# Reordering VectorE and ScalarE work at the first pairs, the half changes and the launch, and making a half's first weight sums within the output projection before it

## The chip, the cores and the metric

The kernel runs on one core of a Trainium2 chip. Its time is the time of one launch on the device, in microseconds. TensorE (PE) does the matrix products, VectorE (DVE) and ScalarE (ACT) prepare their operands and read their results, GpSimd (POOL) takes a few additions, SyncE (SP) issues the loads of the weights. Each engine works through its own list of instructions in the order in which they are written; what has to wait there holds all that stands behind it.

## The reference

One decoding step of a two-layer trunk, for 512 prompt tokens and 64 sample tokens that share all weights (576 tokens, width 1024, everything in float32). Cut to the parts that the change touches:

```python
D_MODEL, D_FF, DEPTH = 1024, 2816, 2

def rms_norm(x, g):
    return x * lax.rsqrt(jnp.mean(x * x, axis=-1, keepdims=True) + EPS) * g

def swiglu(x, w_gu, w_down):
    g, u = jnp.split(x @ w_gu, 2, axis=-1)
    return (jax.nn.silu(g) * u) @ w_down

for l in range(DEPTH):
    x += 0.5 * swiglu(rms_norm(x), w_gu_1, w_down_1)        # half 0, half 2
    if l % 2 == 0:
        x += concat(attention(norm x), pooling(norm x)) @ w_o   # mixer of layer 0
    else:
        x += (Bg * conv3(Cg * v)) @ w_out                   # mixer of layer 1
    x += 0.5 * swiglu(rms_norm(x), w_gu_2, w_down_2)        # half 1, half 3
y = rms_norm(x)
```

So four feed-forward halves are run, in the order half 0, attention mixer, half 1, half 2, convolution mixer, half 3, final norm.

## The kernel before

**Numbers.** Tokens lie on the free axis, as two column halves of 288. A float32 operand is split into a high part (ACT: a cast, L100 for weights, L240 for activations) and a low part (DVE: source minus high part, L101, L241), and a product is made as three: high by high, high by low, low by high. A row of weights can't be used before both its cast on ACT and its difference on DVE are there.

**A unit** (`unit`, one 128-wide slice of gate and up) is done in a Strassen-like form with seven block products instead of eight. They are called B11, T1, B21, B22, T2, T3 and T4 after the form of x that they use, each of twelve matmuls 128x288 (`seven`, L381). B11 and B21 use the raw weights (group "a"), T1 and T2 use the group "e", T3 and B22 the group "f". "e" and "f" are made from sums of weight blocks: three DVE additions, L111 to L113 (`Weights.sums`), then a split each. T4 uses weights split by `dsplit` (tiles dh, dl). It is run in the next unit, once its result bank B has been read by the gate products: the DVE operations L387 and L388 make h from it, and T4 waits for L387. The copy of T2's result (tile u, ACT L475 in the first unit of a chunk) has to be done before T3 writes into the same bank.

**Forms of x.** The products need B11, T1, B21, B22, T2, T3, T4 of x: sums and differences of quarters of x, multiplied by the norm's gain and split. `forms_low` makes those of a row d below 4, `forms_high` and `form_b22` and `forms_main` those of the row d+4. The sum of squares of x for the norm is collected beside them by `square` (ACT L285 squares, POOL L286 adds).

**Order.** 22 units of a half are run in four chunks of 5, 5, 6 and 6. After each chunk's units come eight down projections in the order 0, 4, 1, 5, 2, 6, 3, 7, and x is updated row by row. In the last chunk of a half that is followed by another half, and in the output projection of a mixer, each update of x (L650, L787, L1005) is followed by the forms of the next half. `W.ahead(n)` issues the splits of the next n weight groups at the place where it stands. Groups "e" and "f" need a tile for the sum, `spool`, which before exists only within a half's own pools (`ffn_pools`). So at the two output projections the splits stop short of the first "e".

**Where engines meet.** A chunk's first unit (`unit` with `prev` None) has no unit before it whose products could fill the time in which its operands are made. The first unit of a half is also marked `start`: the norm's factor is made there, `tok_factor` on PE (L327), a square root on ACT (L331), `newton` and `factor_tiles` on DVE, and a turn on PE (L346).

**Launch.** In half 0 the first three units are done in the plain form (`first_pairs`, `plain`, L494), while the forms for the seven products are still made; `late_form` makes T4's form for four rows after the first unit in seven products.

Of the kernel before, what the change touches and what calls it, by code (L numbers as in the profile page):

```python
# [32 lines left out]
C = 288  # L33
# [13 lines left out]
class Weights:  # L47
# [5 lines left out]
    def __init__(self, nc, raw_pool, split_pool, units):  # L53
# [12 lines left out]
        self.spool = self.dpool = None  # L66
# [36 lines left out]
    def sums(self, u):  # L103
# [4 lines left out]
        t = self.sum[u] = self.spool.tile([128, 2048], F32, tag="sum", name="sum")  # L108
# [6 lines left out]
    def split(self):  # L115
# [3 lines left out]
        if k in ("e", "f") and self.spool is None:  # L119
            return  # L120
# [52 lines left out]
class Trunk:  # L173
# [63 lines left out]
    def hi_lo(self, hl, src, g):  # L237

        nc = self.nc
        nc.scalar.activation(out=hl[0], in_=src, func=AF.Copy, scale=g)  # L240
        nc.vector.scalar_tensor_tensor(out=hl[1], in0=src, scalar=g, in1=hl[0].bitcast(F32), op0=ALU.mult, op1=ALU.subtract)  # L241
# [10 lines left out]
    def forms_high(self, k, n, xb, st):  # L252

        ng = self.ngain[:, n, k + 4:k + 5]
        self.form_b21(k, n)
        self.form_t32(k, n, xb, st)
        self.nc.vector.scalar_tensor_tensor(out=st[:, 2], in0=self.x[:, k + 4, :C], scalar=ng, in1=st[:, 1], op0=ALU.mult, op1=ALU.subtract)

    def form_b21(self, k, n):
        self.hi_lo(self.form("B21", k), self.x[:, k + 4, :C], self.gain[:, n, k + 4:k + 5])  # L260
# [10 lines left out]
    def forms_main(self, k, st):  # L271

        n = st.shape[1]
        h, l = (t[:, k, 1:1 + n, :] for t in self.mn)
        self.nc.scalar.copy(out=h, in_=st)
        self.nc.vector.tensor_tensor(out=l, in0=st, in1=h.bitcast(F32), op=ALU.subtract)
# [127 lines left out]
    def unit(self, u, j, prev, fresh, start, pre):  # L404
# [31 lines left out]
        if prev:  # L436
# [19 lines left out]
            return s  # L456
        we = W.take()
# [38 lines left out]
    def plain(self, j, outs, mid={}):  # L496
# [18 lines left out]
    def first_pairs(self, n):  # L515
# [6 lines left out]
        tmp = lambda: tp.tile([128, C], F32, tag="t1", name="t1")  # L522
# [5 lines left out]
        for i, j in ((0, 1), (2, 3), (4, 5), (6, 7), (4, 6), (0, 2), (0, 4)):  # L528
            nc.vector.tensor_tensor(out=sq[i], in0=sq[i], in1=sq[j], op=ALU.add)
        self.hidden_tiles()  # L530
        W.ahead(1)

        def sums(ks):
            for k in ks:
                xb, st = tmp(), tp.tile([128, 3, C], F32, tag="st", name="st")[:, :2]
                nc.scalar.activation(out=xb, in_=self.x[:, k, C:], func=AF.Copy, scale=self.gain[:, n, k:k + 1])
                self.form_t32(k, n, xb, st)
                self.forms_main(k, st)

        (g0, g1), (u0, u1) = p0  # L540
        fa = []
# [1014 lines left out]
```

## Time and profile before

| | |
|---|---|
| median of 3 runs | 2380.42 us (2378.46 to 2380.97) |
| profiled execution | 2382.45 us, its span 2380.6 us |
| mean granted clock of TensorE | 0.971 |
| PE busy | 2239.2 us, 94% |
| DVE, ACT, POOL busy | 1625.9, 928.8, 431.4 us |

A span is the time from the first to the last instruction in the trace. PE is the busiest engine; what the other engines do costs only where PE waits for it. The clock is given as a share of full speed: 1.0 is 2.4 GHz, 0.50 is 1.2 GHz.

### The profile page before, as it was taken

How to read it: one execution, taken by the hardware profiler on the slowest of the kernel's cores; microseconds unless marked ns; L12 is line 12 of the kernel's file. 1: busy time of each engine (PE TensorE's matmuls, PEld its weight loads, DVE VectorE, ACT ScalarE, POOL GpSimd, SP SyncE). 2: the span in 40 equal slices, each digit the busy share in tenths (PEclk: the TensorE clock that was granted, in tenths of full speed). 3: DMA queues.
4: the chain of work that ended last, by engine and by line, in shares of the span. 5: the costliest groups of instructions: out<-in, count | busy, mean ns of one | idle time of the engine just before them, and what ended most of it. 6: DMA issues, size and time to landing. Idle time of an engine off the chain costs nothing.

```text
span 2380.6 us, 39876 instructions
## 1 busy us (share of the span) xinstructions
PE 2239.2 (94%) x16544; PEld 2186.2 (92%) x16544; DVE 1625.9 (68%) x2600; ACT 928.8 (39%) x1606; POOL 431.4 (18%) x444
## 2 busy tenths in 40 slices
PE   8799999999999979999998799999999989999998
PEld 7799999899888879999998799999999989999998
DVE  6676767635667777668596767767664467768584
ACT  5343524323434335334354534343431245335253
POOL 0000101207556530000011001000222210000012
PEclk9899999999999999999999799999999989999999
DMA  3122222443444412222222122222222212222222
GB/s 130 62 83 87 80 91 83 153 137 113 129 134 137 129 54 76 93 81 89 89 85 76 54 88 79 100 89 72 89 90 89 73 54 87 82 98 85 78 88 75
DMA packets 70949, 217.89 MB, mean 92 GB/s; under 512 B 14256, under 2 KB 37808, under 8 KB 54128
## 3 DMA queue, kind: packets, MB, share of 16 engines
q1 hardware_dynamic: 70336, 215.24, 27.3%
q8 instruction: 130, 2.13, 0.4%
q14 instruction: 51, 0.42, 0.1%
q10 hardware_dynamic: 432, 0.10, 0.0%
HBM read 204.22 MB, written 11.10 MB: 90 GB/s over the span
## 4 chain that ended last, share of the span: by engine, by line
PE 47%; DVE 12%; ACT 4%; issue 2%; POOL 0%; POOLq 0%; ACTq 0%; DVEq 0%
PE B L381 11%; PE acc L362 9%; PE A L579 7%; PE F L579 7%; PE F L381 7%; PE A L381 6%; DVE wl L101 2%; ACT wh L100 2%; DVE sum L111 1%; DVE sum L112 1%; DVE exl L241 1%; DVE sum L113 1%; DVE dl L101 1%; DVE x L650 1%; ACT sqt L285 0%
## 5 line engine op out<-in xcount | busy, mean ns | idle before, releaser
L101 DVE TENSOR_TENSOR wl<-raw,wh 128x1024 fp32r<-128x1024 f32 (+3 forms) x305 | 336.2, 1108 | 145.9 <-ACT wh L100 145.7
L100 ACT CAST wh<-raw 128x1024 fp32r<-128x1024 f32 (+3 forms) x305 | 278.6, 916 | 324.2 <-PE F L579 201.7
L402 POOL TENSOR_TENSOR hl<-h,hh 128x576 fp32r<-128x576 f32 x88 | 134.3, 1526 | 1435.6 <-ACT hh L401 1383.5
L101 DVE TENSOR_TENSOR wl<-sum,wh 128x1024 fp32r<-128x1024 f32 x170 | 207.7, 1223 | 30.3 <-ACT wh L100 30.3
L100 ACT CAST wh<-sum 128x1024 fp32r<-128x1024 f32 x170 | 176.2, 1049 | 106.8 <-DVE sum L112 105.9
L381 PE MATMUL A<-exh,wh 128*128 128x288 f32 x680 | 206.2, 303 | 8.2 <-ACT B L435 5.1
L579 PE MATMUL A<-hh,wh 128*128 128x288 f32 x692 | 204.6, 296 | 5.4 <-ACT wh L100 5.4
L381 PE MATMUL B<-xh,wh 128*128 128x288 f32 x680 | 202.0, 297 | 7.8 <-ACT u L475 7.8
L362 PE MATMUL acc<-xh,wh 128*128 128x288 f32 x960 | 208.0, 298 | 1.3 <-DVE x L650 1.3
L381 PE MATMUL A<-exh,wl 128*128 128x288 f32 x680 | 204.8, 301 | 3.4 <-DVE wl L101 3.4
L381 PE MATMUL A<-exl,wh 128*128 128x288 f32 x680 | 205.4, 302 | 0.8 <-DVE exl L241 0.8
L579 PE MATMUL A<-hh,wl 128*128 128x288 f32 x692 | 204.5, 296 | 1.8 <-DVE wl L101 1.8
L362 PE MATMUL acc<-xl,wh 128*128 128x288 f32 x960 | 205.7, 296 | 0.4 <-POOL xl L1406 0.4
L579 PE MATMUL F<-hh,wh 128*128 128x288 f32 x692 | 205.9, 298 | 0.0
L579 PE MATMUL F<-hl,wh 128*128 128x288 f32 x692 | 205.6, 297 | 0.0
L579 PE MATMUL F<-hh,wl 128*128 128x288 f32 x692 | 205.6, 297 | 0.0
L362 PE MATMUL acc<-xh,wl 128*128 128x288 f32 x960 | 205.5, 296 | 0.0
L579 PE MATMUL A<-hl,wh 128*128 128x288 f32 x692 | 204.2, 295 | 0.0
L381 PE MATMUL B<-xl,wh 128*128 128x288 f32 x680 | 200.3, 295 | 0.0
L381 PE MATMUL B<-xh,wl 128*128 128x288 f32 x680 | 200.2, 294 | 0.0
L362 PEld LDWEIGHTS acc<-xh,wh 128*128 128x128 f32 x960 | 154.4, 189 | 5.7 <-issue 2.8
L362 PEld LDWEIGHTS acc<-xl,wh 128*128 128x128 f32 x960 | 154.8, 189 | 0.7 <-POOL xl L1406 0.6
(370 smaller groups left out, 6034.9 us busy)
## 6 DMA issues: line engine op xcount, KB each, us to landing
raw<-in_gu SPq DMA_DIRECT2D x87, 1024.0 KB, 4.9
raw<-in_dn SPq DMA_DIRECT2D x32, 768.0 KB, 4.2
raw<-in_dn SPq DMA_DIRECT2D x32, 640.0 KB, 3.8
raw<-in_wqk SPq DMA_DIRECT2D x12, 1024.0 KB, 5.1
raw<-in_cv SPq DMA_DIRECT2D x12, 1024.0 KB, 4.9
kv<-in_kb SPq DMA_DIRECT2D x32, 256.0 KB, 3.8
kv<-in_vb SPq DMA_DIRECT2D x32, 256.0 KB, 4.7
raw<-in_wv SPq DMA_DIRECT2D x6, 1024.0 KB, 4.9
```

The costliest lines, as they stand in the source:

```text
L100: self.nc.scalar.copy(out=h, in_=src)
L101: self.nc.vector.tensor_tensor(out=l, in0=src, in1=h.bitcast(F32), op=ALU.subtract)
L111: tt(out=b[:, 0:2], in0=r[:, 0:4:2], in1=r[:, 2:4], op=ALU.add)
L112: tt(out=b[:, 2], in0=b[:, 1], in1=r[:, 0], op=ALU.add)
L113: tt(out=b[:, 3], in0=b[:, 2], in1=r[:, 1], op=ALU.add)
L241: nc.vector.scalar_tensor_tensor(out=hl[1], in0=src, scalar=g, in1=hl[0].bitcast(F32), op0=ALU.mult, op1=ALU.subtract)
L362: nc.tensor.matmul(out=p[:, c, :C], lhsT=w, rhs=m[:, k0 + k, c * C:c * C + C], start=(first and k == 0 and z == 0), stop=(last and k == kn ...
L381: nc.tensor.matmul(out=out, lhsT=a[:, v], rhs=m, start=(first and k == 0 and z == 0), stop=(last and k == 3 and z == 2), skip_group_check= ...
L402: nc.gpsimd.tensor_tensor(out=self.hl[:, j, :], in0=s["h"], in1=self.hh[:, j, :].bitcast(F32), op=ALU.subtract)
L579: nc.tensor.matmul(out=p[c][:, :C], lhsT=a, rhs=m[:, k, c * C:c * C + C], start=(k == 0 and z == 0), stop=(k == kc - 1 and z == 2))
L650: tt(out=xd[:, cs[c]], in0=p[c][:, :C], in1=xd[:, cs[c]], op=ALU.add)
```

## The change

Five things are changed, all of them in the order of instructions.

1. In a chunk's first unit the sums for the next unit stand at the front, before T1's weights are taken. They stood behind B21. T2 is run before B22, and at a half's `start` the norm's factor comes after T2.
2. The sum's tile comes from a function, `Weights.stile`. Both mixers set it before their output projection, so that the first sums and the split of "e" are issued before the last row of x is updated, and `W.ahead(2)` behind the projection issues the split of "f". The sums for the half's second unit come right behind it.
3. Within the forms, the subtraction comes first, casts are put together, and `square` comes after the forms instead of ahead of them.
4. In the down projections the last part of both first rows is run before either row is put out, with the next splits between.
5. In `first_pairs` the sums of squares come before the T1 forms, forms are made in pairs, the norm's root and factor come within the third plain product, and `late_forms` makes T4's forms within the first unit in seven products.

```diff
     def forms_low(self, k, n, xb, tmp):
...
+        nc.vector.tensor_tensor(out=tmp, in0=x0, in1=x1, op=ALU.subtract)
         self.hi_lo(self.form("B11", k), x0, g)
+        self.hi_lo(self.form("T1", k), tmp, g)
         nc.scalar.activation(out=xb, in_=x1, func=AF.Copy, scale=g)
-        nc.vector.tensor_tensor(out=tmp, in0=x0, in1=x1, op=ALU.subtract)
-        self.hi_lo(self.form("T1", k), tmp, g)
...
+    def forms_high(self, k, n, xb, st, second):
...
+        parts = [b21, b22] if second else [b21]
+        for hl, src in parts:
+            self.hi(hl, src, g)
         self.form_t32(k, n, xb, st)
...
+        if second:
+            self.main_hi(k, st)
+        for hl, src in parts:
+            self.lo(hl, src, g)
+        if second:
+            self.main_lo(k, st)
...
+        W.sums(u + 1)
         we = W.take()
         self.seven(f, "T1", we, 0, True, False)
         nc.scalar.copy(out=s["p5"], in_=f)
         s["d"] = W.dsplit(u)
         self.seven(a, "B21", wa, 512, False, True)
+        if not start:
+            gate0()
+        W.ahead(1)
+        if extra:
+            extra()
+        self.seven(b, "T2", we, 512, False, False)
         if start:
             fp = self.pair()
             fa = self.tok_factor(fp[1][:, 256:261], (self.sq,), TOKS, later=True)
-        else:
-            gate0()
-        W.ahead(1)
+        nc.scalar.copy(out=u2, in_=b)
+        wf = W.take()
+        self.seven(f, "B22", wf, 512, False, True)
         if start:
             self.newton(*fa)
             ft = self.factor_tiles()
-        W.sums(u + 1)
-        wf = W.take()
-        self.seven(f, "B22", wf, 512, False, True)
-        self.seven(b, "T2", we, 512, False, False)
-        nc.scalar.copy(out=u2, in_=b)
-        if not start:
+        else:
             gate1()
         W.ahead(1)
         self.seven(b, "T3", wf, 0, False, False)
...
     def first_pairs(self, n):
...
-        for k in range(4):
-            t = tmp()
-            nc.vector.tensor_tensor(out=t, in0=self.x[:, k, :C], in1=self.x[:, k, C:], op=ALU.subtract)
-            self.hi_lo(self.form("T1", k), t, self.gain[:, n, k:k + 1])
         sq = [self.sq] + self.sqs
...
         self.hidden_tiles()
         W.ahead(1)
+        for ks in ((0, 1), (2, 3)):
...
-        pg = self.plain(1, self.pair(), {5: lambda: fa.append(self.tok_factor(g1[:, 480:485], (self.sq,), TOKS, later=True))})
+        pg = self.plain(self.pair())
         W.ahead(1)
-        sums((0,))
-        self.newton(*fa[0])
-        ft = self.factor_tiles()
...
+        pu = self.plain((self.bank("B"), self.bank("B")), {1: roots, 5: factors})
         self.plain_out(0, *p0)
...
-                    s = self.unit(u0, j, s, n < 2, i > 0 and ci == 0 and j == 0, last)
+                    extra = (lambda: self.late_forms(self.phases[0][2])) if i == 0 and ci == 0 and j == PLAIN else None
+                    s = self.unit(u0, j, s, n < 2, i > 0 and ci == 0 and j == 0, last, extra)
                     n += 1
-                    if i == 0 and ci == 0 and j == PLAIN:
-                        for k in range(4):
-                            self.late_form(k, self.phases[0][2])
...
+                if e == 1:
+                    for d, p, w in held:
+                        self.down_part(p, w, kc - 1, 1, kc)
+                    self.W.ahead(2)
                 for d, p, w in held:
-                    if e == 1:
-                        self.down_part(p, w, kc - 1, 1, kc)
                     self.down_out(d, p, last, nxt, kind)
...
-        self.square(d, tp)
         if kind == "ffn":
             self.forms(d, nxt, tp)
...
+        self.square(d, tp)
...
             self.open_forms()
+            self.W.stile = lambda: tp.tile([128, 2048], F32, tag="sum", name="sum", bufs=1)
             for d in ORDER:
                 p = self.proj(mh, ml)
                 xd = ch(self.x[:, d, :])
                 nc.vector.tensor_tensor(out=xd, in0=p[:, :, :C], in1=xd, op=ALU.add)
+                self.forms(d, nxt, tp)
                 self.square(d, tp)
-                self.forms(d, nxt, tp)
+            self.W.ahead(2)
```

The attention mixer is given the same lines, with a tile of its own pool; there `forms_high` is called without its second part, and the four rows' `main_hi`, `main_lo` and `form_b22` stand behind the last row.

On DVE, at the first unit of the second chunk of half 0, there stands before (the first row adds the last row of x, L419 is the gate product that uses the first gate, L423 and L424 those of the second, dl belongs to T4's weights):

```order
L647 TENSOR_TENSOR x<-x,dt 128x576
L101 TENSOR_TENSOR wl<-sum,wh 128x1024
L101 TENSOR_TENSOR dl<-raw,dh 128x512
L419 TENSOR_TENSOR g<-A,r 128x288
L101 TENSOR_TENSOR wl<-raw,wh 128x1024
L111 TENSOR_TENSOR sum<-raw 128x1024
L112 TENSOR_TENSOR sum<-sum,raw 128x512
L113 TENSOR_TENSOR sum<-sum,raw 128x512
L423 TENSOR_TENSOR g<-F,u_1239 128x288
L424 TENSOR_TENSOR g<-g,r 128x288
L101 TENSOR_TENSOR wl<-sum,wh 128x1024
```

and at the same place after the change:

```order
L678 TENSOR_TENSOR x<-x,dt 128x576
L101 TENSOR_TENSOR wl<-sum,wh 128x1024
L111 TENSOR_TENSOR sum<-raw 128x1024
L112 TENSOR_TENSOR sum<-sum,raw 128x512
L113 TENSOR_TENSOR sum<-sum,raw 128x512
L101 TENSOR_TENSOR dl<-raw,dh 128x512
L431 TENSOR_TENSOR g<-A,r 128x288
L101 TENSOR_TENSOR wl<-raw,wh 128x1024
L435 TENSOR_TENSOR g<-F,u_1231 128x288
L436 TENSOR_TENSOR g<-g,r 128x288
L101 TENSOR_TENSOR wl<-sum,wh 128x1024
```

The three sums moved up past dl, the first gate product and a weight split; the rest kept its order. This is so at all twelve chunk starts that aren't a half's start.

On DVE, at the end of the convolution mixer's output projection, there stands before (L787 adds a row of x, the first one row 3 and the second one row 7; exl, xl and st are forms):

```order
L787 TENSOR_TENSOR x<-acc,x 128x576
L241 SCALAR_TENSOR_TENSOR exl<-x,gain,exh 128x288
L249 TENSOR_TENSOR t_19456<-x 128x288
L241 SCALAR_TENSOR_TENSOR exl<-t_19456,gain,exh 128x288
L787 TENSOR_TENSOR x<-acc,x 128x576
L241 SCALAR_TENSOR_TENSOR exl<-x,gain,exh 128x288
L268 SCALAR_TENSOR_TENSOR st<-x,gain,xb 128x288
L269 SCALAR_TENSOR_TENSOR st<-x,ngain,st 128x288
L257 SCALAR_TENSOR_TENSOR st<-x,ngain,st 128x288
L241 SCALAR_TENSOR_TENSOR xl<-x,gain,xh 128x288
L276 TENSOR_TENSOR xl<-st,xh 128x864
L111 TENSOR_TENSOR sum<-raw 128x1024
```

and after:

```order
L817 TENSOR_TENSOR x<-acc,x 128x576
L252 TENSOR_TENSOR t_19445<-x 128x288
L246 SCALAR_TENSOR_TENSOR exl<-x,gain,exh 128x288
L246 SCALAR_TENSOR_TENSOR exl<-t_19445,gain,exh 128x288
L111 TENSOR_TENSOR sum<-raw 128x1024
L112 TENSOR_TENSOR sum<-sum,raw 128x512
L113 TENSOR_TENSOR sum<-sum,raw 128x512
L101 TENSOR_TENSOR wl<-sum,wh 128x1024
L817 TENSOR_TENSOR x<-acc,x 128x576
L279 SCALAR_TENSOR_TENSOR st<-x,gain,xb 128x288
L280 SCALAR_TENSOR_TENSOR st<-x,ngain,st 128x288
L265 SCALAR_TENSOR_TENSOR st<-x,ngain,st 128x288
```

The sums and the split of "e" now stand ahead of row 7, and the operation that follows an addition to x directly no longer needs ACT's cast of that row.

On ACT, at the start of half 3, there stands before, from the square of row 7 on (B and p are copies of TensorE's results, fr is the norm's root, u is the copy that T3 waits for):

```order
L285 ACTIVATE sqt<-x 128x576
L240 ACTIVATE exh<-x,gain 128x288
L240 ACTIVATE xh<-x,gain 128x288
L275 CAST xh<-st 128x864
L100 CAST wh<-sum 128x1024 x2
L435 COPY B<-A 128x288
L459 COPY p_19552<-F 128x288
L100 CAST dh<-raw 128x512
L331 ACTIVATE fr<-fr 128x5
L100 CAST wh<-raw 128x1024
L475 COPY u_19553<-B 128x288
```

and after:

```order
L100 CAST wh<-sum 128x1024
L243 ACTIVATE exh<-x,gain 128x288
L243 ACTIVATE xh<-x,gain 128x288
L284 CAST xh<-st 128x864
L297 ACTIVATE sqt<-x 128x576
L100 CAST wh<-sum 128x1024
L447 COPY B<-A 128x288
L472 COPY p_19556<-F 128x288
L100 CAST dh<-raw 128x512
L100 CAST wh<-raw 128x1024
L343 ACTIVATE fr<-fr 128x5
L484 COPY u_19557<-B 128x288
```

The cast of "e" moved ahead of row 7's forms, the square behind them, and the root behind the cast of the next weights.

## Rows read from the trace of the kernel before

**Rows 1.** The page's head and its first part: busy time and instructions.
```profile
span 2380.6 us, 39876 instructions
PE 2239.2 (94%) x16544; PEld 2186.2 (92%) x16544; DVE 1625.9 (68%) x2600; ACT 928.8 (39%) x1606; POOL 431.4 (18%) x444
```

**Rows 2.** Stretches: length, busy time and instructions by engine, clock, DMA share, GB/s.
```profile
0.00:92.00 92.00, 67.79 (x419) 62.27 (x420) 60.69 (x112) 45.05 (x83) 4.88 (x8) 0.87 0.28 92
876.00:908.00 32.00, 17.01 (x103) 15.71 (x103) 24.11 (x39) 15.21 (x27) 2.66 (x2) 0.79 0.10 33
909.00:1276.00 367.00, 357.50 (x2635) 354.69 (x2634) 265.94 (x381) 150.24 (x241) 33.66 (x22) 0.99 0.25 85
1276.00:1344.00 68.00, 48.65 (x289) 45.10 (x289) 48.92 (x78) 30.57 (x53) 9.95 (x7) 0.77 0.17 59
1943.00:1975.00 32.00, 18.71 (x112) 17.06 (x111) 22.14 (x38) 13.55 (x26) 2.81 (x2) 0.78 0.10 33
```

**Rows 3.** Waits of PE: waiting tile and line, releaser: us, times, longest.
```profile
PE B L381 <- DVE h L387: 37.3, 15, 2.6
PE F L381 <- ACT wh L100: 20.5, 3, 11.1
PE B L381 <- ACT wh L100: 10.2, 1, 10.2
PE B L381 <- ACT u L475: 7.8, 16, 0.5
PE F L327 <- DVE sq L529: 6.9, 1, 6.9
PE A L579 <- ACT wh L100: 5.4, 3, 4.9
PE A L381 <- ACT B L435: 5.1, 2, 4.3
```

**Rows 4.** DVE in order of time, a chunk start: start, duration, [idle before].
```profile
140.53 1.22 DVE L111 TENSOR_TENSOR sum<-raw 128x1024 f32<-128x1024 f32 x1
...
142.50 0.69 DVE L113 TENSOR_TENSOR sum<-sum,raw 128x512 f32<-128x512 f32 x1
...
145.50 1.23 DVE L101 TENSOR_TENSOR wl<-sum,wh 128x1024 fp32r<-128x1024 f32 x1 [1.45 <-ACT wh L100]
...
147.13 0.46 DVE L388 TENSOR_TENSOR h<-h,g 128x288 f32<-128x288 f32 x1
```

**Rows 5.** Stretches behind a wait of PE; the clock stands before the DMA share.
```profile
148.60:152.01 3.41, 3.41 (x17) 3.41 (x16) 1.27 (x3) 1.30 (x2) 1.42 (x1) 0.50 0.29 38
351.60:355.00 3.40, 3.40 (x28) 3.40 (x27) 2.95 (x6) 0.94 (x2) 0.00 (x0) 1.00 0.16 19
739.41:742.82 3.41, 3.41 (x30) 3.41 (x31) 2.41 (x9) 0.83 (x2) 3.33 (x2) 1.00 0.39 128
```

**Rows 6.** DVE in order of time, output projection of the convolution mixer.
```profile
1928.00 0.75 DVE L787 TENSOR_TENSOR x<-acc,x 128x576 f32<-128x576 f32 x1
1929.99 1.43 DVE L241 SCALAR_TENSOR_TENSOR exl<-x,gain,exh 128x288 fp32r<-128x288 f32 x1 [1.24 <-ACT exh L240]
...
1942.53 0.75 DVE L787 TENSOR_TENSOR x<-acc,x 128x576 f32<-128x576 f32 x1
...
1957.32 1.23 DVE L101 TENSOR_TENSOR wl<-sum,wh 128x1024 fp32r<-128x1024 f32 x1 [0.43 <-ACT wh L100]
```

**Rows 7.** POOL in order of time, the same place.
```profile
1929.67 1.43 POOL L286 TENSOR_TENSOR sq<-sq,sqt 128x576 f32<-128x576 f32 x1 [6.62 <-ACT sqt L285]
```

**Rows 8.** DVE in order of time, last down projections of half 1.
```profile
1283.36 0.45 DVE L650 TENSOR_TENSOR x<-A,x 128x288 f32<-128x288 f32 x1
...
1297.22 0.45 DVE L650 TENSOR_TENSOR x<-A,x 128x288 f32<-128x288 f32 x1
```

**Rows 9.** DVE in order of time, launch: the late forms.
```profile
79.65 0.45 DVE L566 TENSOR_TENSOR t<-xh,xl 128x288 f32<-128x288 f32 x1
...
86.79 0.46 DVE L570 TENSOR_TENSOR xl<-t,xh 128x288 fp32r<-128x288 f32 x1 [0.50 <-ACT xh L569]
```

More of the change, by code (lines that the diff above doesn't have):

```diff
@@ L107, in sums @@
         r = self.need(u).rearrange("p (b n) -> p b n", b=4)
-        t = self.sum[u] = self.spool.tile([128, 2048], F32, tag="sum", name="sum")
+        t = self.sum[u] = self.stile()
         b = t.rearrange("p (b n) -> p b n", b=4)
@@ L118, in split @@
         u, k = self.groups[self.n_split]
-        if k in ("e", "f") and self.spool is None:
+        if k in ("e", "f") and self.stile is None:
             return
@@ L269, in form_t32, with main_hi, main_lo @@
         stt(out=st[:, 1], in0=self.x[:, k, :C], scalar=ngk, in1=st[:, 0], op0=ALU.mult, op1=ALU.subtract)
[L271 to L275, printed above, removed]
+    def main_hi(self, k, st):
+        self.nc.scalar.copy(out=self.mn[0][:, k, 1:1 + st.shape[1], :], in_=st)
+    def main_lo(self, k, st):
+        h, l = (t[:, k, 1:1 + st.shape[1], :] for t in self.mn)
         self.nc.vector.tensor_tensor(out=l, in0=st, in1=h.bitcast(F32), op=ALU.subtract)
@@ L402, in hidden_parts, with unit @@
         nc.gpsimd.tensor_tensor(out=self.hl[:, j, :], in0=s["h"], in1=self.hh[:, j, :].bitcast(F32), op=ALU.subtract)
-    def unit(self, u, j, prev, fresh, start, pre):
+    def unit(self, u, j, prev, fresh, start, pre, extra=None):
         nc, W, tp, r = self.nc, self.W, self.tp, self.r
@@ L556, in first_pairs, with late_forms @@
         W.ahead(1)
-        p2.append(self.plain(2, self.pair()))
+        sums((2, 3))
+        p2.append(self.plain(self.pair()))
         W.ahead(1)
         self.plain_out(2, *p2)
-    def late_form(self, k, n):
+    def late_forms(self, n):
         nc, tp = self.nc, self.tp
-        t = tp.tile([128, C], F32, tag="t1", name="t1")
-        h, l = (v.bitcast(F32) for v in self.form("T2", k))
-        nc.vector.tensor_tensor(out=t, in0=h, in1=l, op=ALU.add)
-        nc.vector.scalar_tensor_tensor(out=t, in0=self.x[:, k + 4, :C], scalar=self.ngain[:, n, k + 4:k + 5], in1=t, op0=ALU.mult, op1=ALU.subtract)
-        h, l = self.form("T4", k)
-        nc.scalar.copy(out=h, in_=t)
-        nc.vector.tensor_tensor(out=l, in0=t, in1=h.bitcast(F32), op=ALU.subtract)
+        h, l = (t[:, :, 3, :] for t in self.mn)
+        sts = [tp.tile([128, 3, C], F32, tag="st", name="st")[:, :2] for _ in range(2)]
+        for i, st in enumerate(sts):
+            nc.vector.tensor_tensor(out=st, in0=self.mn[0][:, 2 * i:2 * i + 2, 2, :].bitcast(F32),
+                                    in1=self.mn[1][:, 2 * i:2 * i + 2, 2, :].bitcast(F32), op=ALU.add)
+            for k in (0, 1):
+                d = 2 * i + k + 4
+                nc.vector.scalar_tensor_tensor(out=st[:, k], in0=self.x[:, d, :C], scalar=self.ngain[:, n, d:d + 1], in1=st[:, k], op0=ALU.mult, op1=ALU.subtract)
+            nc.scalar.copy(out=h[:, 2 * i:2 * i + 2], in_=st)
+        for i, st in enumerate(sts):
+            nc.vector.tensor_tensor(out=l[:, 2 * i:2 * i + 2], in0=st, in1=h[:, 2 * i:2 * i + 2].bitcast(F32), op=ALU.subtract)
     def down_part(self, p, w, k0, kn, kc):
@@ L663, in forms @@
         else:
[L664 to L667 removed]
+            self.forms_high(d - 4, nxt, self.xb, tp.tile([128, 3, C], F32, tag="st", name="st"), True)
     def final_tiles(self):
@@ L793, in ffn_pools @@
         self.ps = pool("ps", 3, space=PSUM)
-        self.W.spool, self.W.dpool = pool("wsum", 1), pool("wd", 1)
+        spool, self.W.dpool = pool("wsum", 1), pool("wd", 1)
+        self.W.stile = lambda: spool.tile([128, 2048], F32, tag="sum", name="sum")
     def ffn_tiles(self, ctx):
@@ L1001, in run @@
             st = {}
+            t.W.stile = lambda: self.tile("P0", [128, 2048])
             for d in ORDER:
@@ L1011, in run @@
                     st[d - 4] = self.tile("P1", [128, 3, C]) if d == 7 else self.tile("PT", [128, 3, C], bufs=3)
-                    t.forms_high(d - 4, nxt, xb, st[d - 4])
+                    t.forms_high(d - 4, nxt, xb, st[d - 4], False)
+                self.sq(d)
+            for k in range(4):
+                t.main_hi(k, st[k])
+                t.main_lo(k, st[k])
             for k in range(4):
                 t.form_b22(k, nxt)
-            for k in range(4):
-                t.forms_main(k, st[k])
+            t.W.ahead(2)
     def tile(self, tag, shape, bufs=1, dtype=F32):
```

66 lines of the change are left out of this document (38 added, 28 removed).

## The prediction

> **What bounds the kernel now.** I read the page's first part first: PE is busy 2239.2 us of a span of 2380.6, so some 141 us are left in which PE waits [rows 1]. Only those, and the time in which PE runs at a low clock, can be won; DVE and ACT have room over the whole span. Then the stretches. A steady stretch of half 1 has PE busy 357.5 of 367 us at a clock of 0.99. The launch has 67.8 of 92 at 0.87, and the three stretches in which a half follows a mixer or another half have 17.0 of 32, 48.7 of 68 and 18.7 of 32 at 0.77 to 0.79 [rows 2]. Over the four, PE is idle 24.2 + 15.0 + 19.4 + 13.3 = 71.9 us, half of all there is. In them PE's busy time is also long, since part of it goes at 1.2 GHz. With two levels, 0.5 and 1, a stretch of length L and mean clock c has spent 2(1 - c)L at the low one: 23.9 us in the launch, 13.4 at 876, 31.3 at 1276, 14.1 at 1943. Half of what PE does in that time is lost, so at most 12, 6.7, 15.6 and 7 us, less where it stands idle.
>
> Third, who makes PE wait. The longest sum is 37.3 us in 15 waits for h, L387, at most 2.6 each: the first unit of each chunk, T4 waiting for the gate product. The rest is concentrated: three waits for the first "e" weights (20.5: 11.1 at 876, the other 9.4 at 1276 and 1943), one of 10.2 in the launch, 6.9 for the squares in the launch, 5.4 and 5.1 in the half change [rows 3].
>
> **The change part by part.**
>
> *Chunk starts, twelve of them.* At 140 the DVE does L111 to L113 from 140.53 to 143.19, about 2.6 us, then the second gate, then waits 1.45 us for ACT's cast, then splits, and h is done with L387 ahead of 147.13 [rows 4]. It looks as if 2.6 us in front of h were moved away, 12 x 2.6 = 31 us. I don't believe that. The sums are moved, not removed, and they now stand ahead of dl, the first gate product and the split of the second weights, all on the same way to h. DVE has the same work between its last row of x and L387 in both orders. The ACT part has too: gate activation, cast, gate activation, cast. So h comes at the same time, and T4's products start at the same time. What changes is where PE waits: the copy u stands behind the cast that follows the first gate, and that gate now comes 2.6 us later on DVE, so T3 waits longer than its 0.5 [rows 3]. I take 1.7 for T3 and 1.4 for T4, the same 3.1 as 0.5 and 2.6 now. At four starts DVE has some 0.5 us of idle time ahead of dl that the new order fills, by my reading of each start: -2 us. Bounds: -31 (all of the wait goes) to +15 (T3's 1.3 more at each of 12 and T4 as before).
>
> *The clock there.* Behind the wait at 144.5 PE runs 3.41 us at 0.50, so it loses 1.7 us; behind the equal wait at 348 it doesn't, with 1.00 [rows 5]. Counted in the same view, seven of the twelve starts show the low stretch, one of them twice as long: 8 x 1.7 = 13.6 us in all. In the mixer a wait of 2.1 us that ends at 739.41 is followed by 1.00 [rows 5]. With the 3.1 us split into two waits of under 2 with 3.4 us of products between, I expect fewer low stretches. Bounds: 0 to -13.6; I take half, -7.
>
> *Convolution mixer into half 3.* Of the 13.3 us idle between 1943 and 1975 [rows 2], the largest is T1 waiting for "e". In the new order the sums (2.6), the cast's remainder (0.4) and the split (1.2) stand ahead of row 7, so T1 has its weights as soon as row 7's forms let B11 start. That puts 4.2 us ahead of row 7 unless DVE gets rid of as much before. It does. A pair of rows takes it 14.5 us now, 1928.00 to 1942.53 [rows 6], while PE's two projections are 96 matmuls at 357.5/2635 = 0.136 us, so 13.0 at most [rows 2]. DVE is the slower by 1.5 and falls behind over three pairs by some 5 us. Part of its pair is waiting: 1.24 us after each addition for ACT's square and cast, and L241 then takes 1.43 [rows 6], where L570 of the same size takes 0.46 [rows 9], because POOL's addition of 1.43 lies across it [rows 7]. With the subtraction or the st operations first, DVE does 0.45 to 1.6 us of work in that time, and the square comes after the casts. My pair: row addition 0.8, forms 1.7, then ACT's casts and square to 3.4 after the addition, split 1.2; high row 0.8, three st 1.6, two low parts 1.0, the joint low part 1.06, ACT's cast to 4.2, split 1.2: about 11.6, with collisions 12.4. That is under 13.0, so PE sets the pace and row 7 comes about 2 us earlier than now in spite of the 4.2. Behind it the chain to T4 of the first unit is shorter by the second "e" and "f" sums' place: forms 3.8, cast and split "f" 1.9, sums 2.6, dl and split 2.0, where now it is forms 6.2, sums 2.6, splits 2.8 (the first starts at 1957.32 [rows 6]), dl, split, factor, sums again. T4 starts near 1962.5 instead of at the end of the stretch: -12 us, of which about 3 is clock. Bounds -15 (all 13.3 and some clock) to -5 (DVE keeps its 14.5, row 7 comes 4 us later and only the second part of the chain is shortened).
>
> The Trainium skill, "SBUF — State Buffer", section "Who interferes with whom", says that VectorE with two SBUF inputs and a GpSimd operation that reads SBUF take turns on one port pair for a whole instruction, in order of issue. The rows agree: L241 began 0.32 us after POOL's addition and ended 0.3 after it [rows 6, 7]. By that rule the later addition will now lie across the weight split instead of across L241. If every meeting cost the full 0.9 again, the pair would be 13.3 and the term -11.
>
> *Half 1 into half 2.* Here DVE is behind by more: rows come every 13.9 us a pair [rows 8], against 72 matmuls x 0.136 = 9.8. The new order makes it 11.6 to 12 by the same steps, so DVE stays the slower one, but over two and a half pairs it is 5 us ahead. The 4.9 us in which the next down weights' cast stands behind the forms' casts [rows 3] goes, since the splits now come before the first row is put out. T1's wait for "e" (its part of the 9.4, 3.6 us) goes, as does the 4.3 for the copy B [rows 3], which stood behind "f"'s cast. The idle time is 19.4, the clock another 7 or 8, half of the 15.6 above. What replaces it: x's rows 3 and 7 still come late, and the sums stand ahead of row 7. T4, now at the stretch's end near 1344, comes at 1327 to 1330. I take -15; bounds -19 and -8.
>
> *Attention mixer into half 1.* Idle 15.0 us, of which 11.1 is T1's wait for "e" [rows 2, 3]. The sums and split, 4.2 us, are put ahead of row 7, of which 1.4 is idle of DVE today, so row 7 and B11 come 2 us later. Forms behind it stay long, since the four rows' joint forms stand there. T4 earlier by 5 to 10; I take -7.5.
>
> *Launch.* The wait of 6.9 for the squares [rows 3] goes: seven additions of about 0.75 are no longer behind four T1 forms that each wait for ACT. A low stretch behind it goes too, worth up to 3. The second large wait, 10.2 [rows 3], is for weights cast behind the late forms, which take 79.65 to 87.25 one after another [rows 9]. Paired they take about 5.6 (two additions of 0.7, four operations of 0.5, one cast of 0.7 that isn't covered, two low parts of 0.75), but they now stand ahead of u, so T3 waits some 9 us in place of T4's 10.2. DVE, busy 60.7 of 92 [rows 2], has the same work in all and gives some of the first gain back. -8; bounds -12 and -4.
>
> *First rows of the down projections in the last chunks of halves 0 and 2.* A wait of about 1 us each: -2; bounds -2 and 0. The reads of PSUM wait there for one more part on PE, 0.8 us, hidden by the rows still to be put out.
>
> Moved DMA: none is issued elsewhere; the raw tile is free 2.6 us later at a chunk start, since dl frees it. Its successor is used over 15 us later and takes 5 us to land, so nothing waits. Instruction counts differ by a handful.
>
> The sum: -2 - 7 - 12 - 15 - 7.5 - 8 - 2 = -53.5. The profiled execution took 2382.45, which gives 2329. It was 2.0 above the median of 2380.42, so the forecast is 2327.
>
> **The rivals.**
>
> *Only half comes.* DVE stays the bound in the three transitions: collisions move to the splits, and the sums ahead of row 7 turn a wait for "e" into a wait for x. For it: DVE is busy 75% of the stretches at 876 and 72% at 1276 [rows 2]. Against it: the 1.24 us of idle per row [rows 6]. By the near bounds of these terms: -5 - 8 - 5 - 4 - 2 = -24, no clock: 2356.
>
> *Chunk starts gain in full.* h comes 2.6 us earlier because ACT, not DVE, set it: the 1.45 us wait speaks for that [rows 4], the sums' mere moving against it. 31 us in place of 2 and the clock's 13.6 in place of 7: 2291.
>
> *Slower.* At the chunk starts ACT's queue is the mechanism: u stands behind the later gate and cast, T3 slips by up to 2.6, and what ACT does for h is queued behind u and slips with it, so T4 still waits 2.6. PE loses 2.6 + 1.7 of clock at 12 starts, 52 us, and a low stretch at all of them. It decides from the point where this exceeds the gains at the transitions and launch, 44.5: with the half gains of 24 the time is 2380.4 + 28 = 2408, with 44.5 it is 2388. Against it: ACT's casts have 1 to 3 us of idle around them there, and h hangs on ACT only for the gate and the cast.
>
> *The change doesn't do what it says.* If the next raw weights weren't there when the sums come early, DVE would stand and row 7 with it. The wait would be moved to row 7: launch and form order alone, -12: 2368.
>
> **How the numbers follow.** Forecast 0.64, half 0.17, full chunk starts 0.06, slower 0.08, not as it says 0.05. A measurement of this kernel tells about 0.2% from no change, 4.8 us. The forecast's own range, by the sums of the terms' middle bounds, is 2310 to 2344. The half case lies above it, so the range goes to 2358; below it goes to 2306. Faster 0.87, since half the gains still is 1%; same 0.05 and slower 0.08 from the slower case and the low end of the last.
>
> **What would show it.** Right: at chunk starts T3 waits for u 1 to 2 us and T4's wait falls below 2, with the same sum. T1 no longer waits for "e" at any of the three transitions. A pair of rows takes at most 13 us in the convolution mixer and 12 in half 1. L327 doesn't wait for squares in the launch. The mean clock rises above 0.98. Wrong: T4's wait of 2.6 still there beside a longer T3 wait; B11 waiting over 4 us for row 7; the low stretches as many as before.

## The result and the profile after

The changed kernel takes 2320.26 us (median of 4 runs, 2315.53 to 2322.07), the kernel before 2380.69 beside it; the ratio is 0.9745, interval 0.9728 to 0.9762. The forecast was 2327. The profiled execution has a span of 2319.0 us, 61.6 less than before, at a mean clock of 0.986.

The head of the page of the kernel after, which answers to [rows 1]:

```profile
span 2319.0 us, 39839 instructions
PE 2216.7 (96%) x16544; PEld 2167.9 (93%) x16544; DVE 1627.6 (70%) x2596; ACT 925.3 (40%) x1604; POOL 436.7 (19%) x444
```

DVE and ACT work as long as before. PE's idle time fell by 39.1 us (from 2380.6 - 2239.2 = 141.4 to 102.3), and its busy time by 22.5 with the same 16544 matmuls: that is the clock, whose records show 141.7 us at 0.50 before and 67.2 after.

The stretches that answer to [rows 2] (launch, attention into half 1, a steady stretch, half 1 into half 2, convolution into half 3), with the same columns:

```profile
0.00:84.00 84.00, 70.13 (x430) 64.87 (x431) 60.49 (x109) 45.04 (x83) 6.16 (x9) 0.88 0.30 101
861.00:892.00 31.00, 23.54 (x151) 22.12 (x150) 27.70 (x44) 19.74 (x34) 4.38 (x3) 0.89 0.15 46
909.00:1200.00 291.00, 282.17 (x2107) 280.07 (x2106) 211.56 (x304) 115.49 (x184) 24.06 (x16) 1.00 0.26 88
1264.00:1304.00 40.00, 29.83 (x181) 27.38 (x181) 34.37 (x56) 21.34 (x37) 7.27 (x5) 0.83 0.16 53
1897.00:1917.00 20.00, 15.42 (x112) 14.23 (x112) 17.63 (x33) 11.33 (x22) 1.64 (x1) 1.00 0.15 52
```

In the last one PE does the same 112 matmuls as in the stretch at 1943 before, in 20 us instead of 32. The steady stretch, which holds chunk starts, is at 1.00.

Waits of PE after, columns as in [rows 3] (L393 is L381 of before, L399 is L387, L484 is L475, L441 the first matmul of a half, which waits for row 7 of x):

```profile
PE B L393 <- ACT u L484: 25.8, 15, 5.1
PE B L393 <- DVE h L399: 18.8, 14, 1.4
...
PE A L393 <- ACT B L447: 7.1, 4, 2.4
PE F L393 <- ACT wh L100: 4.5, 2, 3.7
...
PE B L441 <- DVE x L1038: 2.9, 1, 2.9
PE B L441 <- DVE x L817: 2.5, 1, 2.5
```

The wait for h fell from 2.6 to 1.4 at the longest, and the wait for u rose: 37.3 + 7.8 before, 18.8 + 25.8 after. The sum hardly moved, but it holds 5.1 us of the launch now; at the twelve chunk starts alone it is 37.3 before and 35.2 after. T1's wait for "e" at the transitions fell from 20.5 to 3.7, all of it in the half change (the other 0.85 of the 4.5 lies in the launch, at 55.97). The wait of 6.9 for the squares of the launch is gone from the list. Row 7 of x is waited for at two transitions, 2.5 at the convolution where it was 4.1, and 2.9 at the attention mixer where it was 0.8.

DVE at the same chunk start as [rows 4], after:

```profile
127.47 1.23 DVE L111 TENSOR_TENSOR sum<-raw 128x1024 f32<-128x1024 f32 x1
...
132.56 1.23 DVE L101 TENSOR_TENSOR wl<-raw,wh 128x1024 fp32r<-128x1024 f32 x1 [1.44 <-ACT wh L100]
...
136.10 1.23 DVE L101 TENSOR_TENSOR wl<-sum,wh 128x1024 fp32r<-128x1024 f32 x1 [1.45 <-ACT wh L100]
137.24 0.45 DVE L399 TENSOR_TENSOR h<-B,p 128x288 f32<-128x288 f32 x1
```

and ACT beside it, in the same form:

```profile
131.50 1.03 ACT L100 CAST wh<-raw 128x1024 fp32r<-128x1024 f32 x1
132.44 0.39 ACT L484 COPY u<-B 128x288 f32<-128x288 f32 x1
```

From the sums' start to h it is 9.8 us now and was 6.1 before, since more stands between them; from the last addition to x it is the same 12 us, and so T4 comes as late as before. T3 waits until u is copied at 132.83, behind the cast. On its way to h DVE stands still twice for a cast of ACT, 1.44 and 1.45 us. And the clock behind that start, which answers to the first line of [rows 5]:

```profile
137.75:141.20 3.45, 3.45 (x26) 3.45 (x27) 2.72 (x4) 1.29 (x2) 0.26 (x1) 1.00 0.00 0
```

None of the twelve chunk starts is followed by a low stretch any more. In this one matmuls start every 0.133 us; in the low one of [rows 5], with 17 matmuls where there are 26 here, they start every 0.240. So a low stretch costs 45% of what PE would do in it, and not half.

The convolution mixer's output projection, DVE, as [rows 6], and POOL, as [rows 7], after:

```profile
1872.36 0.76 DVE L817 TENSOR_TENSOR x<-acc,x 128x576 f32<-128x576 f32 x1 [0.56 <-PE acc L374]
...
1882.91 1.68 DVE L101 TENSOR_TENSOR wl<-raw,wh 128x1024 fp32r<-128x1024 f32 x1 [1.43 <-ACT wh L100]
...
1885.16 0.76 DVE L817 TENSOR_TENSOR x<-acc,x 128x576 f32<-128x576 f32 x1 [0.57 <-PE acc L374]
...
1895.46 1.80 DVE L112 TENSOR_TENSOR sum<-sum,raw 128x512 f32<-128x512 f32 x1
...
1899.57 0.75 DVE L817 TENSOR_TENSOR x<-acc,x 128x576 f32<-128x576 f32 x1
```

```profile
1894.88 1.83 POOL L298 TENSOR_TENSOR sq<-sq,sqt 128x576 f32<-128x576 f32 x1 [3.96 <-ACT sqt L297]
```

A pair of rows takes 12.8 us, and DVE waits for PE at its start: PE sets the pace there, as forecast. L112, one of the sums ahead of row 7, takes 1.80 instead of 0.69 where POOL's addition lies beside it, and that addition is itself 0.4 longer than the 1.43 of [rows 7].

### The profile page after: what moved, and what is told of

The parts are those of the page before. It is cut to its first block, busy times and chain, and to the rows that moved or that the text cites. A ratio compares the mean times of both kernels' runs of the same rounds, so it can differ in the third digit from the quotient of the medians.

```text
span 2319.0 us, 39839 instructions
## 1 busy us (share of the span) xinstructions
PE 2216.7 (96%) x16544; PEld 2167.9 (93%) x16544; DVE 1627.6 (70%) x2596; ACT 925.3 (40%) x1604; POOL 436.7 (19%) x444
## 5 line engine op out<-in xcount | busy, mean ns | idle before, releaser
L101 DVE TENSOR_TENSOR wl<-raw,wh 128x1024 fp32r<-128x1024 f32 (+3 forms) x305 | 350.7, 1155 | 220.5 <-ACT wh L100 220.3
L393 PE MATMUL B<-xh,wh 128*128 128x288 f32 x680 | 203.1, 299 | 25.8 <-ACT u L484 25.8
L393 PE MATMUL A<-exh,wh 128*128 128x288 f32 x680 | 204.4, 301 | 7.3 <-ACT B L447 7.1
L393 PE MATMUL A<-exh,wl 128*128 128x288 f32 x680 | 204.0, 300 | 3.9 <-DVE wl L101 3.9
L393 PE MATMUL A<-exl,wh 128*128 128x288 f32 x680 | 203.8, 300 | 0.0
L393 PE MATMUL B<-xl,wh 128*128 128x288 f32 x680 | 201.6, 296 | 0.0
L393 PE MATMUL B<-xh,wl 128*128 128x288 f32 x680 | 201.5, 296 | 0.0
L393 PEld LDWEIGHTS B<-xh,wh 128*128 128x128 f32 x680 | 128.9, 189 | 29.2 <-ACT u L484 29.2
```

Of the source, the lines that this page charges most:

```text
L101: self.nc.vector.tensor_tensor(out=l, in0=src, in1=h.bitcast(F32), op=ALU.subtract)
L393: nc.tensor.matmul(out=out, lhsT=a[:, v], rhs=m, start=(first and k == 0 and z == 0), stop=(last and k == 3 and z == 2), skip_group_check= ...
```

## The experiments

All times are medians; a kernel's own profile gave the waits. The kernel before, run beside each of them, took 2380.69 to 2381.55 us, so the differences from the changed kernel's 2320.26 hold to about a microsecond. A profiled execution can lie a few us from its kernel's median; where a trace is compared with a trace, the difference of the spans is given. The edits are shown as what they come to, not line by line. The span of time between two fixed places (the end of one stage's matmuls and the first wait at the first chunk start of the next half) is called the passage below.

**u early.** T3's copy ahead of the gate and the cast.

```diff
+        self.seven(b, "T2", we, 512, False, False)
+        nc.scalar.copy(out=u2, in_=b)
         gate0()
         W.ahead(1)
-        self.seven(b, "T2", we, 512, False, False)
-        nc.scalar.copy(out=u2, in_=b)
```

> The changed kernel, but at the twelve chunk starts T2 and its copy u stand ahead of the first gate and of the cast of the next unit's weights, so T3 no longer waits behind that cast. My theory (h and with it T4 come when DVE is through its list, the total of the waits at a start is set by that, and the low clock comes from a long undivided wait): T3's wait of 1.7 us goes to about 0, B11 and T4 of the next unit wait 2.5 to 3.1 us in its place, the sum per start stays at 3.1, and low stretches of 3.4 us come back at some of the twelve starts: 2320 to 2333 us. Rival A (the copy behind the cast is a cost of its own): 1.7 us less at each of twelve starts, 2300. Rival B (the clock depends on the sum of the waits and not on their division): no low stretch comes back, 2320.

Measured 2341.18 us, 20.9 more than the changed kernel. Waits of PE, its profile:

```profile
PE B L393 <- DVE h L399: 30.5, 15, 2.3
PE A L393 <- DVE wl L101: 10.8, 14, 2.5
```

The span at a start after five units holds 0.73 us of waiting in B11 and 2.32 in T4, together 3.05 in place of 1.70 + 1.41 = 3.11. The low clock came back at ten of twelve starts; behind the second start it reads

```profile
228.70:234.39 5.69, 5.69 (x24) 5.69 (x25) 2.67 (x4) 1.29 (x2) 1.16 (x1) 0.50 0.16 22
```

Its 24 matmuls in 5.69 us are 0.24 apart. From one chunk's first matmul to the next chunk's, ten of the twelve starts came out 1.25 to 2.55 us longer than in the changed kernel, and the two without a low stretch came out the same to 0.01. The ten add up to 16.9 us, and the two spans differ by 17.1 (the medians by 20.9; in the other three executions the mean clock was 0.974 and not 0.977). So the same idle time costs some 17 us more when one wait is 2.3 us long than when it is parted. Rivals A and B both fall. By the medians the size was 8 us beyond what I expected.

**h first.** The split of the next unit's "e" behind the operations that make h.

```diff
-        W.ahead(1)
         self.seven(b, "T3", wf, 0, False, False)
...
         if prev:
             self.half_mult(prev)
+            W.ahead(0)
```

(The split follows with the next unit's own `W.ahead(1)`, right behind B11's products.)

> The changed kernel, but at the twelve chunk starts the split of the next unit's e weights stands behind the two operations that make h, in place of ahead of them. My theory (h is late because the rest of DVE's list stands ahead of it; e is needed only two products later): T4's wait of 1.4 us goes, T1 of the next unit doesn't wait for e, T3's 1.7 stays: 12 x 1.4 = 17 us less, 2303. Rival (the wait only moves, since e is then late for T1): 2320.

Measured 2302.64, 17.6 less than the changed kernel. T4's waits of 1.4 are gone, T1 doesn't wait, T3's 1.70 stands. At the chunk start of [rows 4] it is now DVE that waits for PE ahead of h:

```profile
133.86 0.46 DVE L436 TENSOR_TENSOR g<-g,r 128x288 f32<-128x288 f32 x1
134.53 0.46 DVE L399 TENSOR_TENSOR h<-B,p 128x288 f32<-128x288 f32 x1 [0.21 <-PE B L393]
```

The order on ACT is the same as in the changed kernel, so h was late because of what stood ahead of it on DVE: the split of "e", and with it the wait for that split's cast.

**Both.** The two together.

> u early and h first together. My theory: at each start only the next unit's B11 waits, some 0.9 us, for the low part of its weights, which still stands behind the first gate and ACT's cast; 2.2 us less at each of twelve starts, 2294. Rival (the sum of the waits is fixed by the amount of DVE work): 2320.

Measured 2300.77: not the 2294 expected. The profile shows 0.73 us of waiting in B11 for the low part of its weights and 0.33 for the copy B, 1.06 in place of 1.70. From the start of the second chunk's first product to its second unit's T1 it is 16.25 us against 16.57 with h first alone: half of what the waits say. The starts of the matmuls show why. They follow each other every 0.133 us, and the two waits, with the first matmul of B11 that comes 0.1 late, put 1.7 us more between them where 1.06 is listed; the single wait of 1.70 puts 2.0. And 0.29 of the 0.32 is lost again around the third unit's T4: its B21 starts 26.10 us after the chunk's first product, against 26.13. So u early brings next to nothing on top of h first.

**Three.** And the split of the raw weights ahead of the first gate.

```diff
+        W.ahead(1)
         gate0()
-        W.ahead(1)
```

> u early, h first, and the split of the next unit's raw weights ahead of the first gate as well. My theory: no wait over 0.5 us is left at the twelve starts, 3.1 us less at each: 2283. Rival (the sum of the waits is fixed by the amount of DVE work): 2320; between them, if part of the wait reappears at T1 for e: about 2300.

Measured 2291.21, ratio to before 0.9622 (0.9608 to 0.9637); expected 2283. From the second chunk's first product to its second unit's T1 it is 15.07 us against 18.23 in the changed kernel: the 3.1 are gone, and a wait of 0.21 for the copy B is what is left. DVE at that start:

```profile
132.65 1.23 DVE L101 TENSOR_TENSOR wl<-raw,wh 128x1024 fp32r<-128x1024 f32 x1 [0.27 <-ACT wh L100]
133.79 0.45 DVE L431 TENSOR_TENSOR g<-A,r 128x288 f32<-128x288 f32 x1
134.16 0.45 DVE L435 TENSOR_TENSOR g<-F,u 128x288 f32<-128x288 f32 x1
134.65 0.46 DVE L436 TENSOR_TENSOR g<-g,r 128x288 f32<-128x288 f32 x1
135.02 0.45 DVE L399 TENSOR_TENSOR h<-B,p 128x288 f32<-128x288 f32 x1
```

Twelve starts give 8 x 3.1 + 4 x 2.6 = 35 us of wait; the time fell by 29. Along the trace a chunk is 2.88 us shorter at eight starts and 2.17 at four, 31.7 in all. In this execution the launch ended 1.6 us later than in the changed kernel, and the stages from half 0's last chunk to half 1's second took 1.5 more, which leaves about the 28.2 by which the spans differ. What the starts waited for was the order, and not the amount of DVE's work: the rival falls.

**The first unit's order undone.** Sums, T2 and factor as before, at chunk and half starts.

```diff
-        W.sums(u + 1)
         we = W.take()
...
+        W.sums(u + 1)
         wf = W.take()
         self.seven(f, "B22", wf, 512, False, True)
         self.seven(b, "T2", we, 512, False, False)
```

> The changed kernel with the first unit of a chunk in its order of before (sums behind B21, B22 ahead of T2, the factor ahead of T2), at the twelve chunk starts and the three half starts; the launch's first unit keeps the new order. My theory: T4 waits 2.6 us again in one piece and T3 0.5, the sum of 3.1 stays; the low stretches come back at about seven to ten starts (12 to 17 us), and some 2 us at the starts behind six units: 2334 to 2340; the half starts lose up to 3 more. Rival (moving the sums itself brought the time): 12 x 2.6 more, 2351.

Measured 2339.69, 19.4 more; the spans differ by 15.6. Each start has 0.49 and 2.61 us again:

```profile
PE B L393 <- DVE h L399: 36.7, 16, 2.6
```

A low stretch follows five of the twelve. Passages: 1.8 more at the attention mixer, 3.2 in the half change, 2.1 at the convolution. So this part's worth, in the execution that was profiled, is about 7 of clock (1.3 to 1.5 at each of the five), 2 of idle at the starts behind six units and 7 at the half starts. The rival's 2351 isn't there.

**The early sums undone.** `Weights.stile` set only within the halves.

```diff
-            self.W.stile = lambda: tp.tile([128, 2048], F32, tag="sum", name="sum", bufs=1)
...
-            t.W.stile = lambda: self.tile("P0", [128, 2048])
```

> The changed kernel, but the two mixers set no tile for sums, so the first sums and the splits of e and f come when the next half starts, as before. My theory: only the attention and the convolution transitions change. T1 waits for e again, some 9 us in the first and 5 in the second, row 7 comes earlier by 3 to 4 us in each: 8 to 12 us more with the clock, 2330. Rival (the shorter forms alone brought those 9 and 13 us): 2320.

Measured 2336.93, 16.7 more. T1 waits for "e":

```profile
PE F L393 <- ACT wh L100: 22.7, 4, 10.8
```

10.80 at the attention mixer and 5.96 at the convolution; row 7 is waited for 0.85 in place of 2.94 and 2.45. The passages are 4.8 and 6.1 us longer, 10.9 in all, as expected; of the 15.4 by which the spans differ, 3 more stand in the stages ahead of half 1 and 1 in the half change, where nothing was changed.

**The forms undone.** Forms and square in their order of before.

```diff
+        self.hi_lo(self.form("B11", k), x0, g)
+        nc.scalar.activation(out=xb, in_=x1, func=AF.Copy, scale=g)
         nc.vector.tensor_tensor(out=tmp, in0=x0, in1=x1, op=ALU.subtract)
-        self.hi_lo(self.form("B11", k), x0, g)
         self.hi_lo(self.form("T1", k), tmp, g)
-        nc.scalar.activation(out=xb, in_=x1, func=AF.Copy, scale=g)
...
+        self.square(d, tp)
         self.forms(d, nxt, tp)
-        self.square(d, tp)
```

> The changed kernel with the forms and the square in their order of before, in the half change and at both output projections. My theory: a pair of rows takes DVE 14 to 14.5 us again; row 7 comes 4 us later in the convolution mixer and 5 later in the change of half 1 into half 2, with more low clock: 10 to 18 us more, 2330 to 2338. Rival (PE sets the pace there, the order of the forms is hidden): 2320.

Measured 2349.60, 29.3 more, well beyond the 18 expected. DVE in the convolution mixer (the first row of a pair, of the next, and row 7):

```profile
1899.61 0.75 DVE L812 TENSOR_TENSOR x<-acc,x 128x576 f32<-128x576 f32 x1
...
1914.12 0.75 DVE L812 TENSOR_TENSOR x<-acc,x 128x576 f32<-128x576 f32 x1
...
1923.16 0.75 DVE L812 TENSOR_TENSOR x<-acc,x 128x576 f32<-128x576 f32 x1
```

A pair takes 14.5 us again, the sums stand ahead of row 7 as well, and PE waits for it:

```profile
PE B L436 <- DVE x L812: 8.4, 1, 8.4
```

The passages are longer by 1.9, 11.9 and 7.3. Beyond them two waits of 1.65 us at the entry of the mixers became 3.65, since the square stands ahead of the first row's split there too. I had not counted those. Together that is 25.1, as the spans have it (25.0); the medians differ by more.

**The launch undone.** `first_pairs` and `late_form` as before.

```diff
+        for k in range(4):
+            t = tmp()
+            nc.vector.tensor_tensor(out=t, in0=self.x[:, k, :C], in1=self.x[:, k, C:], op=ALU.subtract)
+            self.hi_lo(self.form("T1", k), t, self.gain[:, n, k:k + 1])
         sq = [self.sq] + self.sqs
```

> The changed kernel with first_pairs and the late forms as before; the late forms are run within the first seven-product unit, as in the changed kernel. My theory: the wait for the squares, 6.9 us, and its low stretch come back, part of it is given back later because DVE sets the end of the launch: 8 to 10 us more, 2329. Rival (the launch ends at the same time since DVE sets it alone): 2320.

Measured 2329.37, 9.1 more; the first chunk start is 8.8 us later. The wait for the squares is back with 4.9 us, and u's wait behind the single late forms is 10.0 instead of 5.1:

```profile
PE B L393 <- ACT u L484: 28.3, 13, 10.0
...
PE F L339 <- DVE sq L543: 4.9, 1, 4.9
```

**The held rows undone.** The first two rows put out one by one.

```diff
-                if e == 1:
-                    for d, p, w in held:
-                        self.down_part(p, w, kc - 1, 1, kc)
-                    self.W.ahead(2)
                 for d, p, w in held:
+                    if e == 1:
+                        self.down_part(p, w, kc - 1, 1, kc)
```

> The changed kernel with the first two rows of the down projections put out one after the other, the next splits behind them, as before. My theory: a wait of about 1 us comes back in the last chunks of halves 0 and 2, and in half 1 the wait of 4.9 us for the next down weights comes back, of which DVE's order gives up to half back: 4 to 7 us more, 2325. Rival (those splits are hidden by the shorter forms): 2320.

Measured 2323.62 (2322.48 to 2327.84), 3.4 more; the runs of the two kernels don't overlap, by a hair. A wait of 0.8 us is back in half 0 and in half 2, and in half 1 there are 1.56 + 1.08, where it was 4.9 before and is 1.0 in the changed kernel:

```profile
PE A L610 <- DVE wl L101: 2.7, 3, 1.1
...
PE A L610 <- ACT wh L100: 1.6, 1, 1.6
```

From the last chunk start of each half on, that is 0.5, 0.7 and 2.1 us more for halves 0, 2 and 1, together 3.2 of the 3.4 measured. In half 1 the other orders had taken more than half of the difference.

**Forms and early sums undone together.**

> The changed kernel with both the order of the forms and the early sums undone. Undone alone they cost 29.3 and 16.7 us. My theory: the early sums pay only where the shorter forms have made room for them, so with the old forms nothing is lost by undoing them too; row 7 in the convolution mixer comes 4 us earlier than with the old forms alone and T1 waits for e instead: 2345 to 2354. Rival (two gains that add): 2320 + 46 = 2366.

Measured 2356.66: 36.4 more, between my 25 to 34 and the 46 of two gains that add. In the convolution mixer row 7's wait falls from 8.38 to 4.16, as expected, and T1 waits 5.93 for "e":

```profile
PE F L388 <- ACT wh L100: 22.1, 4, 11.1
...
PE B L436 <- DVE x L811: 4.2, 1, 4.2
```

With the old forms the early sums are worth 3.6 and 2.7 us in the two passages, with the new ones 4.8 and 6.1. They don't need the shorter forms to pay, as I had it, but they pay more with them: 10.9 in all against 6.3.

**Four.** Three, and the square of row 3 behind the cast of the first "e" weights, at the convolution (shown) and in the half change.

```diff
                 p = self.proj(mh, ml)
+                if d == 7:
+                    self.square(3, tp)
...
-                self.square(d, tp)
+                if d != 3:
+                    self.square(d, tp)
```

> The kernel with u early, h first and the raw split first (2291.2 us), and in the change of half 1 into half 2 and in the convolution mixer the square of row 3 stands behind the cast of the first e weights. My theory: without POOL's addition beside it L112 takes 0.7 us and not 1.8, so row 7 is reached 1 us earlier at both places, and about 2 us less in all: 2289. Rival (the addition now lies across the split of e and costs as much there): 2291.

Measured 2287.50 (2286.26 to 2291.31), ratio to before 0.9605 (0.9586 to 0.9624), the fastest of all; three had 2289.24 to 2292.66, so the two overlap. The trace is clear on the cause, if not the median on the gain: between the addition of row 3 and that of row 7 it takes 6.54 us, where three has 7.65, and L112 takes

```profile
1869.78 0.69 DVE L112 TENSOR_TENSOR sum<-sum,raw 128x512 f32<-128x512 f32 x1
```

against 1.81 there. The addition on POOL now lies across the end of the split and the first operation on row 7, which takes 0.88 where it took 0.52, so the rival is right for a third of the 1.1.

## Why the prediction was right, step by step

Measured along the trace, term by term (the launch to the first wait of the second chunk, the passages, and what is left within the halves):

| term | forecast | measured |
|---|---|---|
| launch | -8 | -9.4 |
| chunk starts, waits | -2 | -2.0 |
| chunk starts, clock | -7 | -11.2 |
| attention into half 1 | -7.5 | -9.2 |
| half 1 into half 2 | -15 | -13.6 |
| convolution into half 3 | -12 | -13.4 |
| held rows | -2 | -2 |
| sum | -53.5 | -60.8; the spans differ by 61.6 |

*Chunk starts.* "So h comes at the same time" held to a few hundredths: T3 1.70 and T4 1.41 where I took 1.7 and 1.4, and 1.18 with 1.40 at the starts behind six units, 0.5 less. What I wrote as the reason, that the work ahead of h is the same in both orders, was true of these two orders only. Three shows that the work isn't the bound: with the split of "e" behind h, the copy u ahead of the cast and the raw split ahead of the gate, all of the wait goes. In the rival in which ACT sets h, h comes 2.6 us earlier, and it didn't. There is something in it, though: 2.9 us of the way to h were DVE standing still for two casts of ACT, neither of which h needs, and in three h stands ahead of one and behind only 0.27 us of the other.

*The clock.* This is the term that was mis-sized. I took half of 13.6 because I couldn't say which of the stretches would go. All eight went, and u early brought low stretches back with the same idle time in sum. The 13.6 was too much, too: a stretch of 3.41 us cost 1.25 to 1.57 us and not 1.7, and the double one 2.5, since matmuls are 0.240 us apart at the low clock and 0.133 at the high one. The term is 4.2 us beyond the forecast, more than half of the 7 us by which the forecast was too slow.

*The transitions.* The pair of rows in the convolution mixer came out at 12.8 us, under the 13.0 at which PE sets the pace, with the collision where I put it: across the weight split (1.68 to 1.92 us in place of 1.2) and, which I had not foreseen, across L112 among the sums ahead of row 7. Row 7 comes behind a wait of 2.45, and the passage is 13.4 shorter. At the attention mixer row 7 is waited for 2.1 us longer, as written. The half change is DVE's as forecast, 12.0 us a pair:

```profile
1265.51 0.44 DVE L681 TENSOR_TENSOR x<-A,x 128x288 f32<-128x288 f32 x1
...
1277.48 0.44 DVE L681 TENSOR_TENSOR x<-A,x 128x288 f32<-128x288 f32 x1
...
1279.82 1.22 DVE L111 TENSOR_TENSOR sum<-raw 128x1024 f32<-128x1024 f32 x1
```

But of the three waits that were to go there, 4.9, 3.6 and 4.3 us, the trace after has 1.0, 3.66 and 2.40 left. The wait for "e" stayed because PE is at T1 at 1280.4, while DVE comes to the sums for it only at 1279.82, behind row 3 and its forms, and the cast behind them ends at 1283.97. So the sign "T1 no longer waits for e at any of the three" was right at both mixers and wrong here. That the term still came out at -13.6 is in part luck: the time at the low clock around this change fell from 30.7 us to 13.7, worth up to 7.6, and the waits gave the rest.

*The two mixed terms.* Forms and early sums overlap: undone alone they cost 29.3 and 16.7, together 36.4. My prediction's picture, in which the early sums have to be paid for by shorter forms, gives the right sum with both, and is too strong for the sums alone.

*The launch* was right in its size, and T3's wait in place of T4's came out smaller than written: 5.1 instead of 9. The paired late forms take DVE 4.9 us, the single ones in the same place 7.6, and with those the wait is 10.0 (the launch undone).

The other rivals: the one in which only half comes fell with the transitions, which brought 36 us where 34.5 were forecast; the slower one and the one in which the change doesn't do what it says fell with the waits for u and for "e".

## What to carry to other kernels

When work is moved ahead on a queue, count what stands between it and the thing that is waited for in both orders; if all of it still stands there, only the place of the wait moves, and what is gained is to be sought in an operation that isn't needed for it (here the split of "e", worth 1.4 us at each of twelve starts). The same idle time can cost twice, once as idle and once as clock, and parting a wait by a product or two can save the second cost alone: 17 us here, trace against trace. Gains of edits to one queue are measured by undoing each in the finished kernel and pairs of them together; the single costs added up to 78 us where the whole was 60.

## What was not expected

A collision on DVE and POOL lengthens both: POOL's addition took 1.63 to 1.83 us where an operation of DVE with two inputs had begun before it, and 1.43 where it came first; L112, behind it, went from 0.69 to 1.80. The Trainium skill, "SBUF — State Buffer", section "Who interferes with whom", says that a VectorE operation with two inputs in SBUF contends with a GpSimd operation that reads SBUF, and that the order of issue decides which of them is held up. The trace agrees for both.

The low clock returns at ten of twelve starts with waits of 0.3 to 0.7 and 2.3 us, at seven and five of twelve with 0.5 and 2.6 (before, and with the first unit's order undone), and not once in twelve with waits of 1.2 to 1.7 and 1.4 that are 3.4 us apart. The start of half 1 in the changed kernel, which isn't one of the twelve, still has one: behind a wait of 2.08 us that ends at 880.27 the clock is 0.50 from 881.7 to 885.1. What decides between two starts with equal waits isn't shown.
